# A hybrid attention and MLP layer on one core: tiles at whole kilobytes, longer runs of value products, joined head pairs, relu and square left in PSUM

## The chip, the cores and the metric

The kernel runs on one core of one Trainium2 chip. The metric is device time in microseconds, from the start to the end of one execution; lower is better. Engines are called as in the profile: PE is TensorE's matmul, PEld its weight load, DVE VectorE, ACT ScalarE, POOL GpSimd, SP the engine that issues all DMAs here.

## The reference

One layer of a decoder over 2048 tokens of width 1024, in float32. Cut to what matters:

```python
h = rmsnorm(x, norm_attn)
proj = h @ w_in                       # 2700 columns, for four head groups
# A: stick-breaking attention, 4 heads of 64, strictly causal
# B: sparse attention, 4 heads, one K/V: compressed, selected and window (512) branches,
#    each a softmax with an ALiBi slope, added with sigmoid gates
# C: differential attention, 4 heads: softmax(map 0) - lam * softmax(map 1)
# D: sliding window (128) with sinks, 4 query heads on 2 K/V heads
mix = concat(rmsnorm(A), rmsnorm(B), headnorm(C), rmsnorm(D))
x = x + (mix * g_mix) @ w_out
h = rmsnorm(x, norm_mlp)
x = x + relu(h @ w_up) ** 2 @ w_down  # 4096 wide
return rmsnorm(x, norm_final)
```

## The kernel before

**Dense work.** Each dense product is made of three matmuls on operands split in two: the rounded value (hi) and the rest (lo), as hi*hi, hi*lo and lo*hi. Weights are loaded by SP into one of two `raw` tiles (128 x 1024) and split by ScalarE and by VectorE or GpSimd into `w_hi` and `w_lo` (three of each). Activations stand transposed in `T_hi` and `T_lo`, 128 x 8 x 512, for 512 tokens at a time. Four stages P0 to P3 (`proj`) make the projections; four stages M0 to M3 (`mlp`) make the output projection and the MLP. In M, 32 up projections (`up`) each stream the eight 512-column slices of T against 128-column blocks of w (24 matmuls), and `up_end` makes relu, square, and the split into `u_hi` and `u_lo`: relu out of PSUM into the tile `r`, square in `r`, copy to `u_hi`, all on ScalarE, then the subtraction `u_lo = r - u_hi` on VectorE. Two ups later, down groups of six matmuls stream `w` (512 columns) against 128-column blocks of u, and VectorE adds each group into `acc`. The order is: up, eight down groups, up, and so on. At the end of each M, rows are normed, multiplied with `last_gain` (loaded once, in M0) and stored. These groups share three PSUM banks (`pd`, `PD` = 3); in M3, once all attention is over, the banks of `z` and `t` join them.

**Attention.** For each 128 queries, scores `z` (two matmuls of up to 512 columns) are evicted with slope and mask into `row` tiles, the exponentials are taken there, and an item with the attention's blocks is put in a queue (`item`). The stream `values` takes items in order: four 128 x 128 blocks at a time are transposed into a PSUM tile `t`, which ScalarE evicts into one of `PB` = 3 tiles `PT`. `products` then emits the matmuls of up to `RUN` = 2 such tiles in one go, the last tile first: per block one matmul with 64 columns of V as the stationary operand, which is two instructions in the profile, the two heads of a pair into the two halves of bank `o`'s partitions. A run ends where its item ends, so no run spans two items. In the compressed branch of B and in D each 128 queries have two items, one for each head pair, and `keep_o` evicts 128 columns of `o` for each.

**Order.** One thread of Python generators, called streams, emits all instructions; a planner with a cost of its own for each operation says when a stream's next matmul could start, attention streams go ahead of dense ones, and dense work takes what is left. Each engine then runs its instructions in the order emitted. The planner counts how long a PSUM slot is held.

**Placing in SBUF.** Pools lie one behind the other, tiles rounded up to 32 bytes. The constants begin at byte 16512 of a partition. Over a multiple of 1024 bytes, `T_hi` and `T_lo` begin at 160, `acc` and `nx` at 160, `raw`, `w_hi`, `w_lo`, `u_hi` and `u_lo` at 384, `row`, `qst` (queries), `kst` (keys), `v` and `PT` at 704; slices of T and w begin at multiples of 512 or more from there.

In the profile all matmuls have line 291 (`mm`) or 295 (`tr`), all operations of ScalarE, VectorE and GpSimd line 117, DMAs line 247; tiles are told apart by name. The letter behind `z`, `t` and `o` is the head group, that behind `pd` the stage (P or M). In a matmul's name the moving operand stands ahead of the stationary one.

Of the kernel before, what the change touches and what calls it, by code (L numbers as in the profile page):

```python
# [19 lines left out]
D = 1024  # L20
# [11 lines left out]
QB, RB, PB, WB = 4, 7, 3, 3  # L32
PD, ZB, TB = 3, 2, 2
RUN = 2
# [163 lines left out]
class Trunk:  # L198
# [4 lines left out]
    def __init__(self, ctx, tc, args):  # L203
# [11 lines left out]
        self.dn = ctx.enter_context(tc.tile_pool(name="dn", bufs=1))  # L215
        self.T = (self.dn.tile([128, KD, 512], F32R, name="T_hi", bufs=1),
# [41 lines left out]
    def gains_of(self, name):  # L258

        if name not in self.gain:  # L260
            self.gain[name] = self.const.tile([128, KD], F32, name="gain_" + name)
            self.ld(self.gain[name], dap(getattr(self, name), 0, [[1, 128], [128, KD]]))
        return self.gain[name]
# [37 lines left out]
    def constants(self):  # L301
        V, G, const = self.V, self.G, self.const
        self.ident = const.tile([128, 128], F32, name="ident")
        G.memset(self.ident, 1.0)
        G.affine_select(self.ident, self.ident, [[-1, 128]], OP.is_equal, 0.0, base=0, channel_multiplier=1)
        self.mhalf = const.tile([128, 1], F32, name="mhalf")
        G.memset(self.mhalf, -0.5)
        self.qsc = const.tile([128, 6], F32, name="qsc")
# [17 lines left out]
    def weight_specs(self):  # L326
# [16 lines left out]
        for kind, c in self.phases:  # L343
# [8 lines left out]
            else:  # L352
# [6 lines left out]
                for fc in range(FF // 128 // FC):  # L359
# [4 lines left out]
                    if FC * fc + 3 < FF // 128:  # L364
                        yield kind, c, up(FC * fc + 3)

# [203 lines left out]
    def mlp(self, c):  # L570
# [42 lines left out]
        def up_end(ft, ps):  # L613
# [24 lines left out]
        for fc in range(FF // 128 // FC):  # L638
# [4 lines left out]
            for i in range(4):  # L643
                ts = slice(i * 128, i * 128 + 128)
                ss = self.tile(dn, [128, 2], F32, "nt_ss", 3) if last else None
                for d in range(2):
# [8 lines left out]
                    if last:  # L655
                        r = self.tile(dn, [128, 512], F32, "r", 1)
                        A.activation(r, acc[i][:, ds_], AF.Square, accum_out=ss[:, d:d + 1])
                if last:
                    V.tensor_tensor(ss[:, 0:1], ss[:, 0:1], ss[:, 1:2], OP.add)
                    r = self.rstd(dn, ss[:, 0:1], D, "nt")  # L660
                    for d in range(2):
                        o = acc[i][:, d * 512:d * 512 + 512]
                        V.scalar_tensor_tensor(o, o, r[:, 0:1], self.last_gain[:, d * 512:d * 512 + 512], op0=OP.mult,
                                               op1=OP.mult)
# [11 lines left out]
    def attention_constants(self):  # L676
# [4 lines left out]
        def table(name, w, step, off, window):  # L681
            t = const.tile([128, w], F32, name=name)
# [18 lines left out]
        self.identr = const.tile([128, 128], F32R, name="identr")  # L701
        V.tensor_copy(self.identr, self.ident)

        self.neglam = const.tile([128, 1], F32, name="neglam")
        dl = []
        for a_, b_, nm in ((self.diff_lq1, self.diff_lk1, "l1"), (self.diff_lq2, self.diff_lk2, "l2")):
# [3 lines left out]
            s_ = const.tile([128, 1], F32, name="lams_" + nm)  # L710
            V.tensor_tensor_reduce(u[:, 0, :], u[:, 0, :], u[:, 1, :], 1.0, 0.0, OP.mult, OP.add, s_)
            A.activation(s_, s_, AF.Exp)
            dl.append(s_)
# [3 lines left out]
        self.snk = const.tile([128, 4], F32, name="snk")  # L717
        self.ld(self.snk, dap(self.sinks, 0, [[0, 128], [1, 4]]))
        self.nsnk = const.tile([128, 4], F32, name="nsnk")
# [17 lines left out]
        self.rowok = const.tile([128, 1], F32, name="rowok")  # L737
# [141 lines left out]
    def values(self):  # L879
# [3 lines left out]
        while True:  # L883
# [20 lines left out]
            for g in range(0, nb, 2):  # L904
# [4 lines left out]
                yield self.when([p for P, _ in bl for p in P], "t", TB)  # L909
# [4 lines left out]
                for a, (P, _) in enumerate(bl):  # L914
# [8 lines left out]
                for a, (P, v) in enumerate(bl):  # L923
                    for j in range(len(P)):
                        ops.append((j, v[j], pt[:, 2 * a + j, :], first and g + a == 0, last and g + a == end[j]))
# [650 lines left out]
```

## Time and profile before

| | us |
|---|---|
| median of three timed runs | 3186.9 (3185.98 to 3189.75) |
| the profiled execution, its own time | 3182.32 |
| its span, first to last instruction | 3180.6 |
| PE busy | 3074.8 |
| VectorE busy | 2068.3 |
| ScalarE busy | 1772.9 |
| GpSimd busy | 710.3 |

Busy times are read as shares of the span. A matmul's duration runs from the start of its reading to the end of its result; the next starts long before that, so durations of neighbours overlap, and the distance from one start to the next tells what a matmul costs. In the timeline a row "xN" merges N neighbours of one kind. An attention stage shows as letters A, C, D, B in turn for each 512 queries.

### The profile page before, as it was taken

To read this page: it belongs to the slowest core of one execution; us is meant where nothing else is said; L and a number is where in the kernel's file an instruction comes from. 1 tells how busy PE (TensorE), PEld (TensorE's weight loads), DVE (VectorE), ACT (ScalarE), POOL (GpSimd) and SP (SyncE) were. 2 spreads that over 40 slices of the span, in tenths; PEclk is the share of its full clock that TensorE was granted. 3 is DMA by queue.
4 is the path that set the end of the run, shared out by engine and by line. 5 is a ranking of instruction groups with operands and counts; after the bars stand their busy time and mean duration, and the time that the engine had idled before them with its cause. 6 is when DMAs were issued, how large, how long until landed. Compare 5 with 4: busy or idle time off the path is not lost.

```text
span 3180.6 us, 51156 instructions
## 1 busy us (share of the span) xinstructions
PE 3074.8 (97%) x19152; PEld 2515.3 (79%) x19152; DVE 2068.3 (65%) x4278; ACT 1772.9 (56%) x3459; POOL 710.3 (22%) x479
## 2 busy tenths in 40 slices
PE   8999999999999999989999998999999999999998
PEld 6878887888877777878877776778777778888886
DVE  4774667655758887776566878687665554545545
ACT  4654667554657765656556776566554554333333
POOL 3042313222311222233121112233221112210000
PEclk9999999999999999999999999999999999999999
DMA  7778564765232344364223323452532222423332
GB/s 219 191 196 208 163 164 139 200 179 139 77 94 77 89 112 123 104 175 112 69 75 95 94 75 94 119 168 76 129 110 69 69 69 63 145 86 96 90 100 86
DMA packets 456649, 376.53 MB, mean 118 GB/s; under 512 B 127056, under 2 KB 405712, under 8 KB 454736
## 3 DMA queue, kind: packets, MB, share of 16 engines
q1 hardware_dynamic: 456400, 373.26, 42.6%
q8 instruction: 151, 2.47, 0.3%
q14 instruction: 98, 0.80, 0.1%
HBM read 319.59 MB, written 53.58 MB: 117 GB/s over the span
## 4 chain that ended last, share of the span: by engine, by line
PE 75%; DVE 12%; ACT 6%; DMA 3%; issue 2%; POOL 1%; SPq 1%; DVEq 0%; POOLq 0%; ACTq 0%
PE pdM L291 40%; PE pdP L291 13%; DVE row L117 8%; PE zB L291 4%; PE tB L295 4%; PE oB L291 4%; ACT row L117 4%; PE zC L291 2%; PE oC L291 2%; PE tC L295 2%; DVE acc L117 1%; ACT w_hi L117 1%; DMA raw<-in_w_in_dram 1%; PE tA L295 1%; DMA raw<-in_w_out_dram 1%
## 5 line engine op out<-in xcount | busy, mean ns | idle before, releaser
L117 POOL TENSOR_TENSOR w_lo<-raw,w_hi 128x1024 fp32r<-128x1024 f32 (+1 forms) x188 | 468.6, 2496 | 1363.1 <-ACT w_hi L117 1248.3
L117 ACT ACTIVATE w_hi<-raw 128x1024 fp32r<-128x1024 f32 (+2 forms) x376 | 388.7, 1047 | 462.5 <-PE pdM L291 269.7
L117 DVE TENSOR_TENSOR acc<-acc,pdM 128x512 f32<-128x512 f32 (+1 forms) x576 | 367.8, 652 | 172.3 <-PE pdM L291 162.7
L291 PE MATMUL pdM<-T_lo,w_hi 128*128 128x512 f32 (+1 forms) x1088 | 419.7, 386 | 4.4 <-POOL T_lo L117 4.4
L291 PE MATMUL pdM<-T_hi,w_hi 128*128 128x512 f32 (+1 forms) x1088 | 419.9, 386 | 2.1 <-ACT T_hi L117 1.5
L291 PE MATMUL pdM<-T_hi,w_lo 128*128 128x512 f32 (+1 forms) x1088 | 419.6, 386 | 0.0
L291 PE MATMUL pdM<-w_hi,u_hi 128*128 128x512 f32 x1024 | 405.2, 403 | 8.5 <-DVE acc L117 3.4
L291 PE MATMUL pdM<-w_hi,u_lo 128*128 128x512 f32 x1024 | 405.5, 396 | 3.0 <-DVE u_lo L117 3.0
L291 PE MATMUL pdM<-w_lo,u_hi 128*128 128x512 f32 x1024 | 404.7, 396 | 0.0
L117 DVE TENSOR_TENSOR w_lo<-raw,w_hi 128x1024 fp32r<-128x1024 f32 (+1 forms) x188 | 249.3, 1333 | 220.3 <-ACT w_hi L117 211.9
L117 ACT ACTIVATE row<-row 128x1024 f32<-128x1024 f32 (+7 forms) x292 | 228.6, 803 | 116.3 <-DVE row L117 113.7
L291 PEld LDWEIGHTS pdM<-T_lo,w_hi 128*128 128x128 f32 x1088 | 205.5, 189 | 45.9 <-POOL T_lo L117 5.2
L291 PEld LDWEIGHTS pdM<-T_hi,w_hi 128*128 128x128 f32 x1088 | 205.3, 189 | 42.5 <-ACT T_hi L117 1.8
L291 PEld LDWEIGHTS pdM<-T_hi,w_lo 128*128 128x128 f32 x1088 | 205.6, 189 | 40.3 <-issue 0.5
L291 PEld LDWEIGHTS pdM<-w_hi,u_hi 128*128 128x128 f32 x1024 | 193.1, 189 | 54.1 <-DVE acc L117 8.2
L117 ACT ACTIVATE PT<-tB 128x512 f32<-128x512 f32 (+1 forms) x260 | 134.4, 530 | 168.8 <-PE tB L295 167.2
L291 PEld LDWEIGHTS pdM<-w_hi,u_lo 128*128 128x128 f32 x1024 | 194.1, 190 | 43.2 <-DVE u_lo L117 5.1
L291 PEld LDWEIGHTS pdM<-w_lo,u_hi 128*128 128x128 f32 x1024 | 193.8, 189 | 41.6 <-issue 0.5
L117 ACT ACTIVATE row<-row,c_mn 128x1024 f32<-128x1024 f32 (+4 forms) x192 | 171.6, 896 | 93.3 <-DVE c_mn L117 90.4
L291 PE MATMUL pdP<-T_lo,w_hi 128*128 128x512 f32 x480 | 192.0, 400 | 0.0
L291 PE MATMUL pdP<-T_hi,w_hi 128*128 128x512 f32 x480 | 191.4, 399 | 0.1
L291 PE MATMUL pdP<-T_hi,w_lo 128*128 128x512 f32 x480 | 191.0, 398 | 0.0
(211 smaller groups left out, 6554.4 us busy)
## 6 DMA issues: line engine op xcount, KB each, us to landing
raw<-in_w_up_dram SPq DMA_DIRECT2D x128, 512.0 KB, 4.1
raw<-in_w_down_dram SPq DMA_DIRECT2D x128, 512.0 KB, 3.6
raw<-in_w_in_dram SPq DMA_DIRECT2D x72, 512.0 KB, 5.1
acc<-in_x_dram SPq DMA_DIRECT2D x32, 512.0 KB, 4.8
raw<-in_w_out_dram SPq DMA_DIRECT2D x32, 512.0 KB, 4.5
qst<-qk_qA SPq DMA_DIRECT2D x64, 128.0 KB, 3.4
qst<-qk_qC SPq DMA_DIRECT2D x128, 64.0 KB, 3.4
qst<-qk_qD SPq DMA_DIRECT2D x64, 128.0 KB, 3.2
```

The source lines that it names most:

```text
L117: return f(*a, **k)
L291: self.nc.tensor.matmul(out, a, b, start=start, stop=stop, **k)
L295: self.nc.tensor.transpose(out, a, self.ident[:a.shape[0], :a.shape[0]])
```

## The change

Constants: `PB` from 3 to 6, `RUN` from 2 to 4.

Placing: a tile of the pools `at` and `dn` whose row isn't a multiple of 256 elements goes to a new pool `sm` behind them, as do `gain_*`, `qsc`, `t_cmp` and `rowok`; `ident` and `identr` become one tile, the lambda sums one, `snk` and `nsnk` one, and `last_gain` leaves the constants. The constants are then 12160 bytes, and 16512 + 12160 = 28672 is 28 KB, so that all large tiles (T, w, u, raw, acc, nx, row, qst, kst, v, PT) begin at a multiple of 1 KB.

Items: a block gets a third part `m`, the column block of `o` into which its products go. The compressed branch and D make one item for both head pairs; `keep_o` gets the pair of bounds and evicts 256 columns at once.

MLP: relu and square stay in the PSUM tile `ps`, and `u_hi` and `u_lo` are made from it; the tile `r` is gone, and the squares for the last norm are written to `ps` too. `norm_final` is loaded at the end of every M stage through a `raw` tile, which is given back at the fourth block of rows.

```diff
-QB, RB, PB, WB = 4, 7, 3, 3
+QB, RB, PB, WB = 4, 7, 6, 3
-RUN = 2
+RUN = 4
...
     def tile(self, pool, shape, dt, name, bufs, tag=None):
+
+        if pool in (self.at, self.dn) and math.prod(shape[1:]) % 256:
+            pool = self.sm
...
-        self.ident = const.tile([128, 128], F32, name="ident")
-        G.memset(self.ident, 1.0)
-        G.affine_select(self.ident, self.ident, [[-1, 128]], OP.is_equal, 0.0, base=0, channel_multiplier=1)
+        one = self.row_tile()[:, :128]
+        G.memset(one, 1.0)
+        G.affine_select(one, one, [[-1, 128]], OP.is_equal, 0.0, base=0, channel_multiplier=1)
+        self.identr = const.tile([128, 128], F32R, name="identr")
+        V.tensor_copy(self.identr, one)
+        self.ident = self.identr.bitcast(F32)
...
+                yield "G", c, [(lambda t: t, dap(self.norm_final, 0, [[0, 128], [1, D]]))]
...
+            if self.rawq[0][0] == "G":
+                self.wq.append(self.rawq.pop(0)[2])
+                continue
             yield from self.res["w"].take()
...
-        if c == 0:
-            self.last_gain = self.const.tile([128, D], F32, name="last_gain")
-            self.ld(self.last_gain, dap(self.norm_final, 0, [[0, 128], [1, D]]))
...
-            r = self.tile(dn, [128, 512], F32, "r", 1)
-            A.activation(r, ps, AF.Relu)
-            A.activation(r, r, AF.Square)
-            A.activation(uh, r, AF.Copy)
-            V.tensor_tensor(ul, r, uh.bitcast(F32), OP.subtract)
+            A.activation(ps, ps, AF.Relu)
+            A.activation(ps, ps, AF.Square)
+            A.activation(uh, ps, AF.Copy)
+            V.tensor_tensor(ul, ps, uh.bitcast(F32), OP.subtract)
...
-                        r = self.tile(dn, [128, 512], F32, "r", 1)
-                        A.activation(r, acc[i][:, ds_], AF.Square, accum_out=ss[:, d:d + 1])
+                        A.activation(ps, acc[i][:, ds_], AF.Square, accum_out=ss[:, d:d + 1])
...
+                    if i == 0:
+                        gain, = yield from self.weights()
...
                     self.res["acc"].give()
+                    if i == 3:
+                        self.res["raw"].give()
...
-        for n, (j, v, p, _, _) in enumerate(ops):
-            self.mm(o[64 * j:64 * j + 64, 0:128], v, p, n == starts[j], n == stops[j], share=2)
+        for n, (j, m, v, p, _, _) in enumerate(ops):
+            self.mm(o[64 * j:64 * j + 64, 128 * m:128 * m + 128], v, p, n == starts[j], n == stops[j], share=2,
+                    skip_group_check=True)
...
-                self.item(blocks, [self.vcn], [], self.keep_o(box, "c", pr),
-                          rel=(lambda: self.res["pc"].give()) if pr else None)
+
+            def blocks(vc, pc=pc):
+                return [((pc[:, 2 * m, 0:128], pc[:, 2 * m + 1, 0:128]), (vc, vc), m) for m in range(2)]
+
+            self.item(blocks, [self.vcn], [], self.keep_o(box, "c", (0, 2)), rel=lambda: self.res["pc"].give())
...
-            self.evac(box[nm][:, 128 * pr:128 * pr + 128], o[:, :128])
-            if pr and then:
+            self.evac(box[nm][:, 128 * p0:128 * p1], o[:, :128 * (p1 - p0)])
+            if p1 == 2 and then:
                 self.final(then())
...
-                self.item(blocks, [("vD", c, g)], [], self.keep_o(box, "d", g, f),
-                          rel=(lambda: self.give_rows(1)) if g else None)
+            self.item(blocks, [("vD", c, g) for g in range(2)], [], self.keep_o(box, "d", (0, 2), f),
+                      rel=lambda: self.give_rows(1))
```

## Rows read from the trace of the kernel before

**Rows 1.** The page: the span, its first part (busy time, share and instructions of each engine), and the first line of its fourth part, the chain that ended last, by engine.

```profile
span 3180.6 us, 51156 instructions
...
PE 3074.8 (97%) x19152; PEld 2515.3 (79%) x19152; DVE 2068.3 (65%) x4278; ACT 1772.9 (56%) x3459; POOL 710.3 (22%) x479
...
PE 75%; DVE 12%; ACT 6%; DMA 3%; issue 2%; POOL 1%; SPq 1%; DVEq 0%; POOLq 0%; ACTq 0%
```

**Rows 2.** The view of waits, PE alone: who waited for whom, us in total, times, and the longest.

```profile
PE zC L291 <- DVE c_mn L117: 12.6, 13, 3.1
...
PE zA L291 <- ACT row L117: 6.3, 8, 2.1
...
PE pdM L291 <- DVE acc L117: 4.0, 8, 1.1
...
PE pdM L291 <- ACT u_hi L117: 3.4, 2, 2.3
...
PE pdM L291 <- DVE u_lo L117: 3.0, 4, 1.1
```

**Rows 3.** The timeline of PE in three short stretches, each with a run of products between dense or score matmuls: start, duration, what, and how many.

```profile
2354.25 0.39 PE L291 MATMUL pdM<-w_hi,u_lo 128*128 128x512 f32 x1
2354.57 0.44 PE L291 MATMUL oB<-PT,vcn 128*64 128x128 f32 x4
2354.94 0.50 PE L291 MATMUL pdM<-w_lo,u_hi 128*128 128x512 f32 x1
2355.27 0.40 PE L291 MATMUL pdM<-w_hi,u_hi 128*128 128x512 f32 x1
...
1063.37 0.39 PE L291 MATMUL pdM<-w_lo,u_hi 128*128 128x512 f32 x1
1063.69 1.09 PE L291 MATMUL oA<-PT,v 128*64 128x128 f32 x16
1064.71 0.73 PE L291 MATMUL zA<-kst,qst 128*128 128x512 f32 x2
...
2395.46 0.40 PE L291 MATMUL pdM<-T_lo,w_hi 128*128 128x512 f32 x1
2395.79 1.31 PE L291 MATMUL oB<-PT,v 128*64 128x128 f32 x20
2397.03 0.73 PE L291 MATMUL zB<-kst,qst 128*128 128x512 f32 x2
```

**Rows 4.** The timeline of PE in M3: the first and the last of 15 up matmuls in a row (14 distances), and the first and the last of 38 down matmuls in a row (37 distances).

```profile
2851.20 0.40 PE L291 MATMUL pdM<-T_hi,w_hi 128*128 128x512 f32 x1
...
2854.47 0.40 PE L291 MATMUL pdM<-T_hi,w_lo 128*128 128x512 f32 x1
...
2856.55 0.39 PE L291 MATMUL pdM<-w_lo,u_hi 128*128 128x512 f32 x1
...
2864.94 0.39 PE L291 MATMUL pdM<-w_lo,u_hi 128*128 128x512 f32 x1
```

**Rows 5.** The groups of PE's instructions by shape: one of the three groups of each dense kind with 512 columns (the other two have the same counts); count, busy time, mean of one, idle time before them.

```profile
L291 PE MATMUL pdM<-w_hi,u_hi 128*128 128x512 f32 x1024 | 405.2, 403 | 8.5 <-DVE acc L117 3.4 <-ACT u_hi L117 3.4 <-ACT r L117 1.1
...
L291 PE MATMUL pdM<-T_hi,w_hi 128*128 128x512 f32 x960 | 382.8, 399 | 0.6 <-DVE acc L117 0.6
...
L291 PE MATMUL pdP<-T_lo,w_hi 128*128 128x512 f32 x480 | 192.0, 400 | 0.0
```

**Rows 6.** The groups by shape, of ScalarE and of VectorE: the four steps behind an up projection in M, and the like two on a projection in P, which read PSUM.

```profile
L117 ACT ACTIVATE u_hi<-r 128x512 fp32r<-128x512 f32 x128 | 81.0, 632 | 2.5
L117 ACT ACTIVATE r<-r 128x512 f32<-128x512 f32 x128 | 80.9, 632 | 2.4
...
L117 ACT ACTIVATE r<-pdM 128x512 f32<-128x512 f32 x128 | 74.7, 584 | 8.9 <-PE pdM L291 4.5 <-DVE u_lo L117 4.4
...
L117 ACT ACTIVATE u_hi<-pdP 128x512 fp32r<-128x512 f32 x32 | 18.7, 583 | 4.2 <-PE pdP L291 4.2
...
L117 DVE TENSOR_TENSOR u_lo<-r,u_hi 128x512 fp32r<-128x512 f32 x128 | 97.5, 762 | 76.5 <-ACT u_hi L117 76.5
...
L117 DVE SCALAR_TENSOR_TENSOR u_lo<-pdP,u_hi 128x512 fp32r<-128x512 f32 x32 | 21.9, 685 | 10.3 <-ACT u_hi L117 10.3
```

**Rows 7.** The timelines of PE, ScalarE and VectorE around one up projection in M1: its last matmul, the relu, the copy to u_hi, and the subtraction.

```profile
1605.91 0.40 PE L291 MATMUL pdM<-T_hi,w_lo 128*128 128x512 f32 x1
...
1607.74 0.57 ACT L117 ACTIVATE r<-pdM 128x512 f32<-128x512 f32 x1
...
1609.54 0.63 ACT L117 ACTIVATE u_hi<-r 128x512 fp32r<-128x512 f32 x1
...
1610.98 0.69 DVE L117 TENSOR_TENSOR u_lo<-r,u_hi 128x512 fp32r<-128x512 f32 x1
```

**Rows 8.** The page's sixth part (DMA issues: count, size, median us from issue to landing), and the view by tile: duration shortest, median and longest, first and last start. The transposes of group B's outputs, the last of attention, over the whole span; the matmuls on w_out in a stretch about the start of M3.

```profile
raw<-in_w_out_dram SPq DMA_DIRECT2D x32, 512.0 KB, 4.5
...
L295 PE MATMUL tB<-ident,oS x96: 270/273/332, 336.1 to 2693.4; 128*128 128x128 f32 x96
...
L291 PE MATMUL pdM<-w_hi,T_hi x128: 277/280/285, 2753.3 to 2803.9; 128*128 128x256 f32 x128
```

More of the change, by code (lines that the diff above doesn't have):

```diff
@@ L260, in gains_of @@
         if name not in self.gain:
-            self.gain[name] = self.const.tile([128, KD], F32, name="gain_" + name)
+            self.gain[name] = self.sm.tile([128, KD], F32, name="gain_" + name)
             self.ld(self.gain[name], dap(getattr(self, name), 0, [[1, 128], [128, KD]]))
@@ L681, in table @@
         def table(name, w, step, off, window):
-            t = const.tile([128, w], F32, name=name)
+            t = (self.sm if name == "t_cmp" else const).tile([128, w], F32, name=name)
             for o, n in self.pieces(0, w, 512):
@@ L908, in values @@
                 yield from self.res["PT"].take()
-                yield self.when([p for P, _ in bl for p in P], "t", TB)
+                yield self.when([p for P, _, _ in bl for p in P], "t", TB)
                 self.pa = pa
@@ L913, in values @@
                 n = 0
-                for a, (P, _) in enumerate(bl):
+                for a, (P, _, _) in enumerate(bl):
                     for j in range(len(P)):
@@ L922, in values @@
                 ops = []
-                for a, (P, v) in enumerate(bl):
+                for a, (P, v, m) in enumerate(bl):
                     for j in range(len(P)):
-                        ops.append((j, v[j], pt[:, 2 * a + j, :], first and g + a == 0, last and g + a == end[j]))
+                        ops.append((j, m, v[j], pt[:, 2 * a + j, :], first and g + a == 0, last and g + a == end[j]))
                 if run and (len(run) == RUN or run[-1][-2]):
@@ L932, in products @@
         pa, obox, _, _, first, _, _ = run[0]
-        yield self.when([x for r in run for x in [r[2]] + [v for _, v, _, _, _ in r[3]]], "o" if first else None, 1)
+        yield self.when([x for r in run for x in [r[2]] + [v for _, _, v, _, _, _ in r[3]]], "o" if first else None, 1)
         self.pa = pa
@@ L1125, in blocks @@
                     return [((blk(b),) + ((blk(b + 1),) if b < i else ()),
-                             (v[:, b, :],) + ((v[:, b + 1, :],) if b < i else ())) for b in range(0, i + 1, 2)]
+                             (v[:, b, :],) + ((v[:, b + 1, :],) if b < i else ()), 0) for b in range(0, i + 1, 2)]
                 def fin(o, i=i, h=h, rc=rc, t=t):
@@ L1339, in blocks @@
                     return [((P[0][:, b * 128:b * 128 + 128], P[1][:, b * 128:b * 128 + 128]),
-                             (v[:, b0 + b, :], v[:, b0 + b, :])) for b in range(nb)]
-                self.item(blocks, [("vw", c)], [], self.keep_o(box, "w", pr), rel=lambda: self.give_rows(2))
+                             (v[:, b0 + b, :], v[:, b0 + b, :]), 0) for b in range(nb)]
+                self.item(blocks, [("vw", c)], [], self.keep_o(box, "w", (pr, pr + 1)), rel=lambda: self.give_rows(2))
             segs = self.pieces(0, n, 1024)
@@ L1483, in sinks_window, with blocks, f @@
-                self.item(blocks, [("vD", c, g)], [], self.keep_o(box, "d", g, f),
-                          rel=(lambda: self.give_rows(1)) if g else None)
+            def blocks(*v, rw=rw, b0=b0, nb=w // 128):
+                return [((rw[:, 2 * g, b * 128:b * 128 + 128], rw[:, 2 * g + 1, b * 128:b * 128 + 128]),
+                         (v[g][:, b0 + b, :], v[g][:, b0 + b, :]), g) for g in range(2) for b in range(nb)]
+            def f(box=box, mn=mn, sm=sm, t=t, i=i):
+                if t == 3:
+                    self.res["v"].give(2)
+                es = self.small(4, "d_es")
+                V.tensor_tensor(es, self.snk, mn, OP.add)
+                A.activation(es, es, AF.Exp)
+                V.tensor_tensor(sm, sm, es, OP.add)
+                V.reciprocal(es, sm)
+                s_ = box["d"]
+                yield self.when([s_], "t", TB)
+                self.pa = pa
+                ps = self.tt()
+                for r in range(2):
+                    self.tr(ps[:, r, :], s_[:, r * 128:r * 128 + 128])
+                self.res["oS"].give()
+                on = self.on_tile()
+                V.tensor_tensor(on.rearrange("p (h d) -> p h d", d=64),
+                                ps[:, 0:2, :].rearrange("p r (j d) -> p (r j) d", d=64),
+                                es[:, :, None].to_broadcast([128, 4, 64]), OP.mult)
+                self.group_norm_store(on, i, 3)
```

65 lines of the change are left out of this document (17 added, 48 removed).

## The prediction

> **What bounds the kernel now.** I read the page first: of a span of 3180.6 us TensorE (PE) is busy for 3074.8, VectorE for 65% and ScalarE for 56%, and 75% of the chain that ended last lies on PE [rows 1]. A busy PE need not be a PE at its peak, so I read next what PE waited for: the largest entries shown are 12.6 us for scores on VectorE's minima and 6.3 for scores on rows, and the waits of the MLP on its own evictions are 4.0, 3.4 and 3.0 us [rows 2]. So PE has nearly always something to issue, attention or dense work, and time is won where PE's own work shrinks. That can happen in two ways: fewer or cheaper switches between kinds of matmul, and shorter distances between matmuls of one kind. For both I read PE's timeline and take distances from start to start, since durations overlap.
>
> The profiled execution took 3182.3 us (span 3180.6); the median of the three timed runs is 3186.9, 4.6 above it. I make the sum on the profiled one and add the 4.6 at the end.
>
> **Value runs of up to four banks.** Each product is two instructions, four for a block of two heads. The timeline has product runs of 4, 16 and 20 instructions between matmuls of 512 columns [rows 3]. From start to next start: run of 4, 0.37 us (2354.57 to 2354.94); 16, 1.02 (1063.69 to 1064.71); 20, 1.24 (2395.79 to 2397.03). The slopes are 0.65/12 = 0.054 and 0.22/4 = 0.055 us, so four instructions are 0.218 of the 0.37, and 0.152 is fixed. The run's start also comes 0.32 us after the dense matmul ahead of it, where 0.227 is usual (0.093 more), and the first matmul behind the run of 4 takes 0.33 (0.103 more). Together a run costs 0.348 us of PE whatever its length.
>
> How many runs go, I count from the code. A run never spans two items, so an item of b banks has ceil(b/2) runs before and ceil(b/4) after. Stick-breaking: 40 to 24 for each of 2 head pairs. Differential: 24 to 16 for each of 4 heads. Selected branch: 40 to 24 for each of 2 pairs; window branch: 28 to 16 for each of 2. Compressed branch, two items of one block made one: 32 to 16. Sinks: 32 to 16. The sum is 376 to 224, 152 less. Some runs stand back to back today already and cost nothing extra, as the 20 do, which is a run of 16 and one of 4 [rows 3]; I take off a tenth, an estimate. 152 x 0.9 x 0.348 = **48 us less**. All of it is PE time, and nothing hides it. The bounds: 30 us if a third already stands back to back, 53 if none does.
>
> Behind a longer run waits what PE does next, at most 32 instructions instead of 16, another 0.9 us; PE itself loses nothing by that, but VectorE and ScalarE get a score later. The value stream's last bank is still being evicted when a run is emitted, as now; the planner lets other work go first. Six PT buffers leave two beyond a run of four, so no transpose waits for a product. One eviction for two heads' pairs in place of two saves ScalarE time, which bounds nothing here.
>
> **SBUF at multiples of 1 KB.** An up projection streams T (it begins 160 bytes over a multiple of 1 KB) against blocks of w; a down projection streams w (384 bytes over) against blocks of u. Both are 128 x 512 in the same type. In the last stage the up matmuls start every (2854.47 - 2851.20)/14 = 0.2336 us and the down ones every (2864.94 - 2856.55)/37 = 0.2268 [rows 4]. The difference of 6.8 ns holds over long stretches where nothing is waited for. After the change T, w, u, kst and qst all begin at whole kilobytes, so T lies at least as evenly as w does now, and T and w stand to each other as w and u do now. Either way of seeing it gives T the spacing of w. There are 3 x 960 such matmuls in M and 3 x 480 in P [rows 5]: 4320 x 6.8 ns = **29 us less**. That the address makes the difference is my inference; the trace of before has no T at another address. Bounds: nothing, if something else sets the two apart; 50 us more, if going from multiples of 128 bytes to 1 KB is worth another such step for all 4320 + 3072 matmuls of 512 columns. I take the 29 because the row of w is the nearest.
>
> A rule speaks against this term. In the Trainium skill, SBUF — State Buffer, section "SBUF: two separate sides", TensorE has read ports of its own and never waits on another reader. By it the tile's place could buy nothing and the sum would lack this term; it leaves unexplained why the two spacings differ in rows 4.
>
> **Relu and square in PSUM.** Before, an up's bank is free when the relu has been read out of it; after, when VectorE has made u_lo. ScalarE gets faster: an activation out of PSUM takes 584 ns, one from SBUF 632, so the square falls by about 48 and the copy to 583, as u_hi from pdP has it; the subtraction goes from 762 to about 685, as the like one from pdP [rows 6]. That is 0.17 us off a chain that PE hardly waits for: nothing on the end. The price is the bank. In one up of M1 the last matmul starts at 1605.91 and ends about 1606.30; the relu is over at 1608.31, u_lo at 1611.67 [rows 7]. The bank is held 5.4 us instead of 2.0. There are three such banks, and the down groups that follow (six matmuls of 0.227, 1.36 us) then rotate over two. The planner knows the hold and issues attention meanwhile, and in M3, once attention is done, the z and t banks join: 32 of the 128 ups cost nothing. For the other 96 I let today's waits on acc, u_hi and u_lo, 10.4 us [rows 2], nearly double: **8 us more**. Bounds: 0 (cover holds), and 3.4 us x 96 = 326 if nothing covers.
>
> **The gain vector through the raw buffers.** It is loaded once per M stage instead of once, and holds one of two raw buffers until the fourth block of the last group. The next stage's w_out tiles, queued behind it on SP, come in through one buffer. A load lands in 4.5 us [rows 8]. At two of the three borders attention runs and covers; at the last, M2 to M3, nothing does (the last attention transpose is at 2693.4, the first matmul on w_out at 2753.3 [rows 8]). **4 us more**, between 0 and three landings, 14.
>
> **The rest.** Identity from one tile, merged small constants, and u, r and gains in other pools change no instruction of weight. The one added hop at the start (identity cast on VectorE) lies beside the first loads. With 77 us less PE work, VectorE's and ScalarE's chains have less time: their shares rise by a fortieth, and PE will wait a bit oftener. I give back a tenth, **7 us**. More is not likely: attention ends 60 us before M3 begins to use it, so its pace may lag by most of the gain before the end moves.
>
> **Sum.** -48 - 29 + 8 + 4 + 7 = -58; 3182.3 - 58 = 3124, and with the 4.6 **3129 us**. With its own uncertainties 3112 to 3150.
>
> **Rivals.**
> First, the spacing of T has another cause than the address. Then 29 us stay away: 3158. For it: no row shows one tile at two addresses. Against: same shape, type and count, and a steady difference.
>
> Second, whole kilobytes are worth more than w's place now: another 6.8 ns on 7392 matmuls, 50 us, gives 3079. For it: w's 0.2268 us need not be the floor. Against: no row has a 512-column stream that runs steadily faster.
>
> Third, slower than before: the pd bank becomes the bound. Each of 96 ups holds its bank 3.4 us longer; if PE idles one of them, 96 us come in place of the 8, and 3129 - 8 + 96 = 3217. It decides from 0.7 us per up, where 66 us and the 8 eat the gain. For it: three banks, a VectorE queue with instructions of over a microsecond ahead of u_lo. Against: today's waits on these evictions are 4.0 us in all [rows 2], and attention stands ready in these stages. The Trainium skill bears on it: ScalarE: Activation LUTs, "Step-by-step: what each stage is for", calls PSUM the quicker place for ScalarE but useful only where TensorE doesn't need most of PSUM. [...]
>
> Fourth, the change does not make longer runs, because the value stream flushes when its queue is empty. It flushes between items only, and the count above takes that in; I give it no chance of its own.
>
> **How the numbers follow.** Forecast 0.56, first rival 0.22, second 0.13, third 0.09. The likeliest gives 3129. The range reaches down past the second rival with less costs, 3070, and up to the first with its costs doubled, 3158 + 19, say 3180; the third, and what lies below, is left out. A measurement of this kernel tells about 0.2% (6.4 us) from no change: slower than 3193 is most of the third rival, 0.08; within 3180.5 to 3193 fall its mild form and the first rival's worst, 0.05; faster 0.87.
>
> **What would show it.** Runs right: product runs of up to 32 instructions between dense matmuls, 0.35 us fixed each. Alignment right: up matmuls start every 0.227 us, not 0.234; lower still for both kinds would be the second rival. Banks wrong: PE's waits on VectorE's u_lo and acc in the hundreds. Gain vector: a wait on raw from w_out near the start of M3. The forecast is wrong if T still starts every 0.234 us, or if PE's waits grow by more than 40 us.

## The result, and the profile after

The changed kernel takes 3163.4 us in the median of six runs (3159.16 to 3167.26), against 3186.4 of the kernel before: a ratio of 0.9925, 95% interval 0.9912 to 0.9939. That is 23 us less, where 58 were forecast. The direction is right, the size less than half. The profiled execution took 3159.2 us.

The page of the changed kernel, its span and first part, which answer to [rows 1]:

```profile
span 3157.4 us, 50995 instructions
...
PE 3027.8 (96%) x19152; PEld 2533.0 (80%) x19152; DVE 2072.5 (66%) x4278; ACT 1760.3 (56%) x3410; POOL 714.3 (23%) x479
```

The view of cores of the same kernel, span and mean granted clock:

```profile
core 0: 3157.4 us, clock 0.989
```

PE's busy time fell by 47.0 us (3074.8 to 3027.8); its idle time, span less busy, rose from 105.8 to 129.6, by 23.8. Their sum is the 23 us. The forecast had 77 us less work and 19 us of costs. The clock record of the traces divides the busy time further. PE was busy for 47.3 us in stretches of half clock (1.2 of 2.4 GHz) before, and for 56.4 after. Counted at full rate, that is with half of these stretches taken off, PE's work fell from 3051.2 to 2999.6 us, by 51.6, and half clock cost 4.6 more than before.

PE's waits in the changed kernel (us in total, times, longest), which answer to [rows 2]:

```profile
PE pdM L296 <- DVE acc L117: 14.9, 13, 3.1
...
PE pdM L300 <- DVE nx L117: 10.6, 3, 7.0
PE zC L296 <- DVE c_mn L117: 10.2, 12, 3.0
PE zA L296 <- ACT row L117: 8.9, 12, 1.5
PE pdM L296 <- ACT u_hi L117: 6.3, 4, 3.4
PE pdM L296 <- DVE u_lo L117: 5.6, 7, 1.9
```

The three waits of the MLP on its own evictions (acc, u_hi, u_lo) went from 10.4 to 26.8 us, and one wait of 7.0 us on nx, between M3's output projection and its first up, is new.

PE's timeline in M3: the first and last of 48 up matmuls in a row, then of 38 down matmuls; they answer to [rows 4]:

```profile
2848.71 0.39 PE L296 MATMUL pdM<-T_hi,w_hi 128*128 128x512 f32 x1
...
2859.36 0.39 PE L296 MATMUL pdM<-T_hi,w_lo 128*128 128x512 f32 x1
```

```profile
2840.10 0.39 PE L296 MATMUL pdM<-w_lo,u_hi 128*128 128x512 f32 x1
...
2848.48 0.39 PE L296 MATMUL pdM<-w_lo,u_hi 128*128 128x512 f32 x1
```

Ups now start every 10.65/47 = 0.2266 us, downs every 8.38/37 = 0.2265: T has the spacing of w, and neither went lower.

A long run of products in M1, and four transposes without a run ahead of them, which answer to [rows 3]:

```profile
1062.33 0.39 PE L296 MATMUL pdM<-T_lo,w_hi 128*128 128x512 f32 x1
1062.65 1.97 PE L296 MATMUL oA<-PT,v 128*64 128x128 f32 x32
1064.55 0.66 PE L300 MATMUL tA<-identr,row 128*128 128x128 f32 x4
1064.96 0.71 PE L296 MATMUL zA<-kst,qst 128*128 128x512 f32 x2
```

```profile
964.01 0.60 PE L300 MATMUL tB<-identr,row 128*128 128x128 f32 x4
964.36 0.42 PE L296 MATMUL zA<-kst,qst 128*128 128x128 f32 x2
```

From the dense matmul to the transposes are 2.22 us. Less 0.227 for the dense matmul and 32 x 0.0545 for the products, 0.25 are left; the four transposes behind the run take 0.41 instead of 0.35. A run ahead of transposes thus costs 0.31 us, not the 0.348 read between dense matmuls. Counted over PE's whole timeline, neighbouring product rows taken together, there were 398 runs before and are 264 now. Of the 134 that went, 104 had a transpose behind them (235 before, 131 after).

The MLP's evictions in the changed kernel, grouped by shape (ScalarE's relu and square together, its copy, VectorE's subtraction), which answer to [rows 6]:

```profile
L117 ACT ACTIVATE pdM<-pdM 128x512 f32<-128x512 f32 x256 | 149.2, 583 | 12.6 <-PE pdM L296 10.1
L117 DVE TENSOR_TENSOR u_lo<-pdM,u_hi 128x512 fp32r<-128x512 f32 x128 | 87.7, 686 | 64.5 <-ACT u_hi L117 64.2
L117 ACT ACTIVATE u_hi<-pdM 128x512 fp32r<-128x512 f32 x128 | 76.3, 597 | 2.6
```

583, 597 and 686 ns, where some 584, 583 and 685 were forecast. One side in PSUM is enough for ScalarE: before, relu took 584 from PSUM into SBUF, and the last norm's square, whose source `acc` lies in SBUF, went from 631 into SBUF to 591 into PSUM. One up in M1, its last matmul, relu, square, copy and subtraction, which answer to [rows 7]:

```profile
1605.78 0.39 PE L296 MATMUL pdM<-T_hi,w_lo 128*128 128x512 f32 x1
...
1606.99 0.58 ACT L117 ACTIVATE pdM<-pdM 128x512 f32<-128x512 f32 x1
1607.78 0.59 ACT L117 ACTIVATE pdM<-pdM 128x512 f32<-128x512 f32 x1
1608.40 0.60 ACT L117 ACTIVATE u_hi<-pdM 128x512 fp32r<-128x512 f32 x1
...
1611.16 0.68 DVE L117 TENSOR_TENSOR u_lo<-pdM,u_hi 128x512 fp32r<-128x512 f32 x1
```

The bank is held from 1606.17 to 1611.84, 5.7 us, where 5.4 were forecast.

SP's issues about the border from M2 to M3 in the changed kernel, and the view of windows there (us, busy time of PE, PEld, DVE, ACT and POOL with their instructions, granted clock, DMA share, GB/s), which answer to [rows 8]:

```profile
2713.94 0.33 SPq L252 DMA_DIRECT2D raw<-in_norm_final_dram  x1
2716.20 0.38 SPq L252 DMA_DIRECT2D raw<-in_w_out_dram  x1
...
2723.03 0.38 SPq L252 DMA_DIRECT2D raw<-in_w_out_dram  x1
...
2744.22 0.43 SPq L252 DMA_DIRECT2D raw<-in_w_out_dram  x1
```

```profile
2710.00:2735.00 25.00, 20.93 (x99) 17.08 (x98) 12.93 (x20) 12.22 (x23) 13.48 (x10) 0.93 0.38 126
2735.00:2760.00 25.00, 21.98 (x160) 21.29 (x159) 13.46 (x23) 6.71 (x12) 2.52 (x4) 0.93 0.73 232
2760.00:2785.00 25.00, 25.00 (x210) 25.00 (x210) 10.34 (x19) 6.54 (x8) 1.10 (x2) 1.00 0.37 107
2785.00:2810.00 25.00, 18.01 (x142) 17.77 (x141) 10.32 (x16) 10.02 (x15) 12.39 (x10) 0.86 0.13 43
```

The same issues in the kernel before:

```profile
2734.31 6.28 SPq L247 DMA_DIRECT2D raw<-in_w_out_dram  x3
...
2763.30 1.53 SPq L247 DMA_DIRECT2D raw<-in_w_out_dram  x2
```

The gain vector does take a raw buffer: behind it only two w_out tiles are issued ahead of a pause of 21 us. But the pause is not the gain's: before, three tiles were issued and then came one of 23 us. And idle time is paid twice: where PE waits (busy for 18.01 of 25 us), the granted clock falls as well (a mean of 0.86; 1.00 where PE is busy throughout). There the clock is at half from 2792.0 to 2798.8, and the wait on nx ends at 2795.97.

### The profile page after: what moved, and what is told of

Same layout as the page of the kernel before. It is cut to its first block, busy times and chain, and to the rows that moved or that the text cites. A ratio compares the mean times of both kernels' runs of the same rounds, so it can differ in the third digit from the quotient of the medians.

```text
span 3157.4 us, 50995 instructions
## 1 busy us (share of the span) xinstructions
PE 3027.8 (96%) x19152; PEld 2533.0 (80%) x19152; DVE 2072.5 (66%) x4278; ACT 1760.3 (56%) x3410; POOL 714.3 (23%) x479
## 4 chain that ended last, share of the span: by engine, by line
PE 49%; DVE 10%; ACT 5%; DMA 2%; issue 2%; POOL 0%; SPq 0%; DVEq 0%; ACTq 0%; POOLq 0%
PE pdM L296 36%; DVE row L117 7%; ACT row L117 3%; PE zB L296 2%; PE tB L300 2%; PE oB L296 2%; PE zC L296 1%; DVE acc L117 1%; PE tC L300 1%; PE oC L296 1%; ACT w_hi L117 1%; PE oA L296 1%; DMA raw<-in_w_out_dram 0%; PE pdM L300 0%; DVE w_lo L117 0%
```

## The experiments

Each was timed beside the kernel before, whose median was 3185.2 to 3186.5 us in these comparisons. The planner writes a new order for nearly every edit. The three kernels with another placing alone, and the one with five PT buffers, keep PE's order of their base but for 0 to 36 of its 19152 instructions; the others differ from theirs in some 1,900 to 5,500.

The theory going in (theory 1) was that the bank's hold by relu and square costs much more than the 8 us forecast. Its rivals: the gain vector's load (theory 2), and long runs that give their gain back in waits (theory 3).

### The placing

The kernel before with its tiles at multiples of 1 KB:

```diff
+        self.sm = ctx.enter_context(tc.tile_pool(name="sm", bufs=1))
+        pad = self.const.tile([128, 80], F32, name="pad")
...
+        if pool in (self.at, self.dn) and math.prod(shape[1:]) % 256:
+            pool = self.sm
```

> The kernel before with nothing but the placing changed: a pad of 320 bytes behind the constants and the small tiles in a pool of their own, so that T, w, u, raw, acc, nx, row, qst, kst, v and PT begin at multiples of 1 KB; instructions in the same order up to a few dozen. If the tile's place sets the spacing of T and PE is the bound: up matmuls every 0.227 us instead of 0.2336 and 25 to 29 us less than before, 3158 to 3162. If PE's freed time is lost to waits: 10 to 15 us less. If the place does nothing: no change.

3167.7 us (0.9944, 0.9931 to 0.9956): 18 less, between the first two expectations. PE busy 3058.3, idle 106.4, so hardly any of the freed time went to waits. The first and last of 26 ups in M3 are 5.67/25 = 0.2268 us apart:

```profile
2854.45 0.39 PE L296 MATMUL pdM<-T_hi,w_hi 128*128 128x512 f32 x1
...
2860.12 0.39 PE L296 MATMUL pdM<-T_lo,w_hi 128*128 128x512 f32 x1
```

With one order the two traces can be laid beside each other, matmul by matmul. 3856 of the 4320 ups are followed, at full clock and without a wait, by another up. Their distances sum to 911.4 us before and 893.3 here: 18.1 less, 4.7 ns each. The downs gain 3.1 us. The 256-column matmuls lose 4.0: the median of their distances goes from 0.117 to 0.120 us.

Then the changed kernel with T at a multiple of 1 KB, and everything behind it 32 bytes on (384 in the second, with 96 columns for the 8):

```diff
+        pad = self.dn.tile([128, 8], F32, name="pad", bufs=1)
```

> The changed kernel (3163) with one tile of 32 bytes put behind T: T stays at a multiple of 1 KB, and acc, nx, raw, w and u lie 32 bytes over one. The order of PE's instructions stays. Theory A, a moving operand's own address decides, and 32 bytes over a multiple of 64 is what is slow: up matmuls (T moving) stay at 0.227 us, down matmuls (w moving) go from 0.227 to about 0.233; 3072 of them at 5.4 to 6.8 ns are 17 to 21 us, so 3180 to 3184. Theory B, the place of T against w decides, as both explain the kernel before: ups go back to 0.233, downs stay at 0.227, and what the alignment gave is lost, 18 us: 3181. The total does not tell A from B, the two spacings do. Theory C, neither matters: 3163 and no spacing moves.

> As the kernel with w 32 bytes on, but with 384 bytes behind T: acc, nx, raw, w and u lie 384 bytes over a multiple of 1 KB, as raw, w and u did in the kernel before; T stays at 0. Theory A, a multiple of 64 is all that counts: ups and downs both at 0.227, 3163. Theory B, the place of T against w decides: ups at 0.233, 3181. Theory D, whole kilobytes slow the matmuls of 256 columns, which start every 0.1195 us in the changed kernel and every 0.117 in the one before: they go back to 0.117, and 2688 of them at 2.5 ns give 6.7 us, 3156.

3181.0 us (0.9987, 0.9978 to 0.9997) and 3180.3 (0.9980, 0.9969 to 0.9991). M3 with 32 bytes, 48 ups and then 44 downs:

```profile
2861.95 0.40 PE L298 MATMUL pdM<-T_hi,w_hi 128*128 128x512 f32 x1
...
2872.92 0.40 PE L298 MATMUL pdM<-T_hi,w_lo 128*128 128x512 f32 x1
```

```profile
2829.89 0.39 PE L298 MATMUL pdM<-w_hi,u_lo 128*128 128x512 f32 x1
...
2839.63 0.39 PE L298 MATMUL pdM<-w_lo,u_hi 128*128 128x512 f32 x1
```

and with 384 bytes, 48 ups:

```profile
2861.65 0.40 PE L298 MATMUL pdM<-T_hi,w_hi 128*128 128x512 f32 x1
...
2872.61 0.39 PE L298 MATMUL pdM<-T_hi,w_lo 128*128 128x512 f32 x1
```

Ups are back at 10.97/47 = 0.2334 and 10.96/47 = 0.2332 us, though T has not moved; downs, whose w and u both moved, stay at 9.74/43 = 0.2265. Theory B holds: what counts is where T stands against w, the moving operand against the stationary one, and 17 to 18 us hang on it. Theory D falls: with 384 bytes the 256-column matmuls don't go back to 0.117 us but to 0.119. With 32 bytes they do go back, though, so their pace too hangs on the places, and not in the way of the ups. These three comparisons are firm, since the order is the same.

### Relu and square: PSUM or SBUF

The tile r back, paid for with one PT buffer; and the changed kernel with five PT buffers alone:

```diff
-QB, RB, PB, WB = 4, 7, 6, 3
+QB, RB, PB, WB = 4, 7, 5, 3
...
-            A.activation(ps, ps, AF.Relu)
-            A.activation(ps, ps, AF.Square)
-            A.activation(uh, ps, AF.Copy)
-            V.tensor_tensor(ul, ps, uh.bitcast(F32), OP.subtract)
+            r = self.tile(dn, [128, 512], F32, "r", 1)
+            A.activation(r, ps, AF.Relu)
+            A.activation(r, r, AF.Square)
+            A.activation(uh, r, AF.Copy)
+            V.tensor_tensor(ul, r, uh.bitcast(F32), OP.subtract)
```

> The changed kernel with relu and square taken back into the SBUF tile r (one buffer); PB is 5 to make room. The dense matmuls of M wait 28 us longer in the changed kernel than before, and the planner, which counts the hold of a PSUM bank, places dense work elsewhere. Theory 1 (the pd bank held through relu, square, copy and subtraction ate the gain): 15 to 25 us less than the changed kernel (3163), some 3140, and PE's waits on acc and u_hi fall from 21 us back to about 8. Theory 2 (the gain vector in the raw buffer) or theory 3 (long runs delay attention): within 5 us of the changed kernel.

> The changed kernel (3163) with five PT buffers in place of six; relu and square stay in PSUM. The kernel with the tile r in SBUF has five too, for want of room, so its 18 us may belong to the buffers. Theory 1, the PSUM bank's hold: 3163 to 3166, the fifth buffer alone changes little. Rival, a sixth buffer lets transposes run ahead and take PE from other work at a bad time: 3145 to 3150, and the hold costs nothing.

3145.3 us (0.9873, 0.9859 to 0.9887) and 3165.0 (0.9931, 0.9915 to 0.9946). So the bank seemed to cost 18 to 20 us; the fifth buffer changes nothing, not even PE's order. But the waits did not fall as expected: acc and u_hi together went from 21.2 to 11.5 us, not to 8, and all three from 26.8 to 19.7. The same edit the other way in the kernel before, and in that one aligned:

> The kernel before (3186) with one edit: relu and square of an up projection stay in PSUM, and the tile r goes. Theory 1, the bank that is held until u_lo is made costs PE what it cost in the changed kernel, 18 us: 3204, with waits of dense matmuls on VectorE's acc grown from 4 us to 10 or more. The forecast's term: 8 us, 3194. Theory 3, the hold costs only where runs are long, since they keep ScalarE and VectorE busier: 3186 to 3190.

> The kernel before with its tiles at multiples of 1 KB (3168) and relu and square in PSUM. At the old placing this edit cost some 5 us, in the changed kernel some 18. Theory 1a, it is the faster PE that bares the hold, since down groups come sooner to a bank: 3168 + 15, some 3183. Theory 1b, it is the joined items and the rest of the change that bare it: 3168 + 5, some 3173.

3191.1 us (1.0017, 1.0007 to 1.0026) and 3174.1 (0.9959, 0.9944 to 0.9974): 5 and 6 more than their bases, though the waits on acc grew as the theory has it (4.0 to 14.6 us, 3.6 to 15.9). No theory so far gave both 18 and 5.

### Runs and items

Runs of two (`RUN = 2`) in the changed kernel, and with r in SBUF:

> The changed kernel with RUN = 2 (PB stays 6, joined items stay). By the fixed 0.348 us per run, some 120 runs come back: 42 us more than the changed kernel, 3205, if the long runs earn what was forecast. Theory 3 (long runs keep the chain of scores waiting and give the gain back): only 10 to 20 us more, 3175 to 3183, and PE's waits on scores and rows fall.

> The kernel with relu and square in the SBUF tile r and five PT buffers (3145), and runs of at most two PT tiles in place of four. It is the long runs' worth where no PSUM bank is held by the MLP's squares. Theory 1, runs are worth what PE's busy time fell by (31 us from runs of two to four in the changed kernel) and half of it was lost there to waits on held banks: 3145 + 27 to 31, 3172 to 3176. Theory 2, longer runs give only some 16 us wherever they stand, since they cost waits of their own: 3145 + 16 = 3161. The forecast's price, 0.348 us for each run, would give 3145 + 40 = 3185.

3179.9 us (0.9982, 0.9970 to 0.9993) and 3159.3 (0.9922, 0.9908 to 0.9935): with runs of four the time is 16 and 14 lower, each time between two orders. PE's busy time falls by 31.4 (3059.2 to 3027.8, 115 runs fewer) and 31.1 (3053.4 to 3022.3, 98 fewer), 0.27 and 0.32 us a run; at full rate its work falls by 29.9 and 23.7, 0.26 and 0.24 a run. Idle time grows by 14 in both, and the waits on scores, which theory 3 had fall with short runs, are about the same (22.3 us with runs of two, 23.8 with four). Runs of three with r in SBUF:

> The kernel with r in SBUF and runs of up to three PT tiles; with two it takes 3159, with four 3145. Theory 1, PE's own saving and its longer waits both grow with the runs' length: between the two, 3150 to 3154. Theory 2, the waits come from runs of four alone, with one spare buffer of five: 3140 to 3144. Theory 3, the waits come already with three and the fewer runs don't: 3159 or more.

3157.3 us (0.9908, 0.9890 to 0.9925); PE busy 3031.9, idle 119.1 against 103.4 with runs of two and 117.5 with four. The work falls with each step, the idle time jumps at the first. Then the two branches with an item for each head pair again, with r in SBUF and with PSUM:

```diff
-                return [((pc[:, 2 * m, 0:128], pc[:, 2 * m + 1, 0:128]), (vc, vc), m) for m in range(2)]
-            self.item(blocks, [self.vcn], [], self.keep_o(box, "c", (0, 2)), rel=lambda: self.res["pc"].give())
+            for m in range(2):
+                def blocks(vc, pc=pc, m=m):
+                    return [((pc[:, 2 * m, 0:128], pc[:, 2 * m + 1, 0:128]), (vc, vc), 0)]
+                self.item(blocks, [self.vcn], [], self.keep_o(box, "c", (m, m + 1)),
+                          rel=(lambda: self.res["pc"].give()) if m else None)
```

(and the same for D).

> The kernel with r in SBUF (3145), and the compressed branch and the sinks with an item for each head pair again, as in the kernel before; runs of up to four. Theory 1, joined items earn 0.35 us for each of the 32 runs that they save, on the path in full: 3145 + 11 = 3156, which is also what is left between the aligned kernel before and the one with runs of two when alignment and the gain vector are taken off. Rival, they earn nothing that shows (the branches are small and their runs stand back to back with others): 3145 to 3148, and the 11 us belong to something else.

> The kernel with r in SBUF and an item for each head pair (3161), with relu and square in PSUM. The hold of the bank cost 5 to 6 us in the two kernels with the old items, whose gain vector is loaded once, and 18 to 20 in those with joined items and a gain load in each stage. If joined items bare it: 3161 + 5, some 3166. If the gain load, or the rest of the new kernel, does: 3161 + 18, some 3179.

3160.7 us (0.9922, 0.9907 to 0.9937) and 3171.8 (0.9948, 0.9936 to 0.9961). With joined items the time is 15 us lower with r in SBUF and 7 in PSUM (3171.8 to 3165.0); PSUM is 11 slower here, between both expectations. These are differences of two orders too, so what joined items earn in time is not shown; PE's work at full rate falls by 10.2 and 16.0.

### The gain vector

No load of the gain; the last multiplication reads a table that is there anyway, so the output lacks the final norm's gain:

```diff
-                yield "G", c, [(lambda t: t, dap(self.norm_final, 0, [[0, 128], [1, D]]))]
...
-                        V.scalar_tensor_tensor(o, o, r[:, 0:1], gain[:, d * 512:d * 512 + 512], op0=OP.mult,
+                        V.scalar_tensor_tensor(o, o, r[:, 0:1], self.t_causal[:, d * 512:d * 512 + 512], op0=OP.mult,
```

> The changed kernel without the loads of norm_final: the last product takes a slice of a constant table of the same shape instead, so the output lacks the final gain; no raw buffer is held at the end of an M stage. Theory 2 (the held raw buffer starves the next stage's w_out): 10 to 15 us less than the changed kernel, most of it between 2700 and 2800 us, where PE waits 3.0 us on w_hi and 7.0 on nx. Theories 1 and 3: 0 to 5 us less.

3160.8 us (0.9921, 0.9907 to 0.9936), 2.6 below the changed kernel, where theory 2 had 10 to 15. The order differs as well, so the time alone decides little. Between 2690 and 2830 us PE's waits are 14.0 us in the changed kernel and 9.3 without the load; the 3.0 on w_hi are gone, the 7.0 on nx stay. But they are 10.0 with r in SBUF, where the gain is loaded too. Theory 2 falls as the large cost; whether the load costs anything is not shown.

### The order

Does the added idle time come from a plan that is too tight? A margin of 0.5 us with runs of four and of two, and a hop of 0.35 in the third:

```diff
-    HOP, MARGIN = 0.15, 0.1
+    HOP, MARGIN = 0.15, 0.5
```

> The kernel with r in SBUF, runs of four (3145, PE idle 117 us of its span), and the planner's margin from 0.1 to 0.5 us: an attention matmul is taken only when its operands have been ready for that long by the plan, and dense work goes first. The plan counts nothing for the start of a run, so each run that goes takes 0.35 us of unplanned time from ScalarE and VectorE. Theory W, the waits that long runs add come from an order planned too tight: PE's idle time falls by 8 to 14 and the time to 3131 to 3138. Rival, VectorE and ScalarE lack the capacity in these stages: the waits only move, 3143 to 3150.

> The kernel with r in SBUF and runs of two (3159, PE idle 103 us of its span), with the same margin of 0.5 us. Theory W: here the unplanned 0.35 us of many runs already give the slack, so the margin brings little, 3155 to 3160, and runs of four beat runs of two by some 25 us once both have it. Rival: the margin helps both alike, or neither, and the difference stays at 14.

> The kernel with r in SBUF, runs of four (3145), and the time that the planner counts from one engine's result to another's start from 0.15 to 0.35 us, for dense work and for the chains of ScalarE and VectorE too. Theory W: a plan that is less tight everywhere takes away waits on acc and u_lo as well; 3130 to 3140. Rival, no capacity: 3143 to 3150.

3143.0 us (0.9858, 0.9843 to 0.9873), 3183.5 (0.9990, 0.9981 to 0.9999) and 3162.1 (0.9917, 0.9903 to 0.9931). PE's idle time is 120.2, 122.5 and 132.7 us: more slack in the plan gave more idle time, not less. Theory W falls. A loss of 24 us from a margin, with runs of two (3159.3 to 3183.5), fits no theory, so the last question was what an order alone is worth. Margin 0.12 in place of 0.10, with r in SBUF and in the changed kernel:

> The kernel with r in SBUF (3145) with the planner's margin from 0.10 to 0.12 us, a change too small to mean anything but another order of instructions. It measures how far an order alone moves the time. If the order is a small matter: 3142 to 3148. If it is not, this kernel lies 5 us or more from 3145.

> The changed kernel (3163) with the planner's margin from 0.10 to 0.12 us, beside the same edit of the kernel with r in SBUF. If the hold of the PSUM bank costs 18 us whatever the order, this one lies 15 to 20 us above that one. If the 18 were in part the luck of two orders, the difference is under 10 or over 25, and the cost of the hold is known only as a mean over pairs: 18, 20 and 11 so far in the new kernel's pairs.

3157.9 us (0.9918, 0.9904 to 0.9932) and 3146.0 (0.9872, 0.9855 to 0.9890). The one got 13 us slower, the other 17 faster, and their sign is turned round: here PSUM is 12 us faster. The page's first part, with r in SBUF and margin 0.10, and the view of its cores:

```profile
PE 3022.3 (96%) x19152; PEld 2527.3 (80%) x19152; DVE 2059.9 (66%) x4278; ACT 1766.4 (56%) x3410; POOL 714.0 (23%) x479
```

```profile
core 0: 3139.8 us, clock 0.992
```

The same two with margin 0.12:

```profile
PE 3036.7 (96%) x19152; PEld 2539.8 (80%) x19152; DVE 2068.7 (66%) x4278; ACT 1767.0 (56%) x3410; POOL 718.3 (23%) x479
```

```profile
core 0: 3156.1 us, clock 0.986
```

And the page's first part of the changed kernel with margin 0.12, whose span is 3147.1 us at a clock of 0.989:

```profile
PE 3021.7 (96%) x19152; PEld 2529.7 (80%) x19152; DVE 2056.9 (65%) x4278; ACT 1760.6 (56%) x3410; POOL 709.8 (23%) x479
```

Between the first two nearly all of the 16.3 us of span are busy time (14.4), and that is the clock: PE was busy at half clock for 37.4 and 68.8 us, half of the difference is 15.7, and at full rate the work is 3003.6 and 3002.3. But these are single executions. The granted clock changes from one execution of a kernel to the next (0.988 to 0.992 in the four with margin 0.10, 0.986 to 0.990 in the six with 0.12), and at 0.988 and 0.989 the first kernel took 3147.8 and 3146.5, the second 3155.9 and 3158.0. So 8 to 12 of the 13 us are there at one clock as well, and their cause is not shown. The profiled executions of the changed kernel's two orders are 10 us apart, not 17: 6 of them busy time and 4 idle, with one clock. So the theory that the bank's hold costs 18 us falls: that pair compared two orders. What can be said of the hold is a mean over six pairs, PSUM less SBUF: 20 (with five PT buffers in both), 21, 11, -12, 5, 6, on average 8 with an uncertainty of some 5 (their scatter is 12; the last two pairs have nearly the same orders and count for little more than one). That alone doesn't tell 8 from nothing. PE's idle time is steadier: 14, 13, -1, 6, 4, 6 more in PSUM, on average 7 with an uncertainty of some 2.

## Why the prediction was right in direction and wrong in size

**Alignment, 29 forecast, 18 measured: the mechanism right, the term mis-sized.** The spacing did go from 0.2336 [rows 4] to 0.2266 us in M3, as forecast, and the first rival falls; that the time lies near its 3158 is chance. The step that failed is the price: 6.8 ns were read in a steady stretch of M3 and taken for all 4320 matmuls. In the kernel with another placing alone the mean distance of neighbouring ups (those less than 0.26 us apart, at full clock) falls from 0.2331 to 0.2267 us behind 2800 us, where no attention is left, but only from 0.2330 to 0.2287 ahead of it. Over the 3856 neighbours it is 4.7 ns, 18.1 us. The other ups have a transpose, a score, a run or a wait behind them and gain little more than 1 us together: ahead of a transpose the median is 0.231 before and 0.232 after. The sum also left out the 256-column matmuls, which lost 4.0 us; the downs gained 3.1. PE's work at full rate fell by 16.7. Why the gain is smaller beside attention is open. "T and w stand to each other as w and u do now" was the right one of the two reasons given. What the Trainium skill says in SBUF — State Buffer, "SBUF: two separate sides", of other readers on which TensorE never waits, no run here shows; where TensorE's own two operands stand to each other was worth 4 to 7 ns a matmul, and of that the section says nothing.

The second rival (whole kilobytes worth more) falls with 0.2265 us as the lowest steady spacing seen, and with the 256-column matmuls, which got slower.

**Runs and items, 48 forecast, 35 measured.** The difference was counted right, 134 runs fewer for 137, but partly by luck: there were 398 and 264 runs, where the code gave 376 and 224. The step that failed is the price again. It was read from one run of four between dense matmuls, and three quarters of the runs that went stood ahead of transposes, where 0.31 is read. The whole trace gives less than either: from the aligned kernel to the changed one PE's work at full rate fell from 3034.5 to 2999.6, by 34.9 us, 0.26 for each run. For runs of two to four, in pairs, it fell by 29.9, 23.7 and 38.4 us (0.26, 0.24 and 0.34 a run), the time by 16, 14 and 41 (the third pair with margin 0.5). This measure hardly depends on the order: it moved by 1.2 and 3.1 us between two orders of one kernel. The forecast's lower bound, a third back to back, is 152 x 2/3 x 0.348 = 35, not 30.

**Costs, 19 forecast (8, 4 and 7), 28 measured in this order.** 23.8 are idle time; 4.6 are half clock, which the forecast left out. Relu and square in PSUM agree with the forecast's 8 on average, in time (8, uncertain by 5) and in PE's idle time (7, uncertain by 2), and in no order they cost what the third rival gave. That rival's "4.0 us in all" is the wait on acc alone; the three waits are 10.4, as the term itself had it. The gain vector, 4, can't be told from nothing. The tenth given back to waits, 7, is the weakest term: with longer runs PE's idle time grew by 14 in two pairs and shrank by 2 in a third.

**The sum.** Of the 35 us between the forecast's 58 and the measured 23, 12 are the alignment term (29 less 16.7), 13 the runs and items (48 less 34.9), 5 the idle time and 5 half clock.

**The order, not forecast at all.** Any edit here makes the planner write another order, and two orders of one kernel differ by 13 and 17 us. The changed kernel is one draw; with the margin at 0.12 the same kernel takes 3146, 39 less than before instead of 23.

What stays open: why longer runs raise PE's idle time in some orders (neither more margin nor one more PT buffer took it away), what the two orders of one kernel differ by at one clock, and whether the kernel before is a lucky or an unlucky draw; no other order of it alone was timed.

## What to carry to other kernels

Read a spacing in every stage where its matmuls stand before you take it as a price for all of them, not in the steadiest stretch alone, and count the other shapes that a new placing touches; and read the price of a switch ahead of the operation that follows it most often, not in the tidiest example. In a program that a planner orders, time the same kernel under a second order before giving any difference under some 20 us a cause: a comparison of times is firm only if the order stays. Where it can't stay, divide the time into PE's work at full rate, half clock and idle time, and compare each. Give the two operands of a 512-column matmul the same place over a multiple of 1 KB, and look at both together, not at each alone; the 256-column matmuls here lost by it, so count both kinds.

## What the runs showed of the hardware that was not expected

TensorE's pace in fp32r depends on where its two SBUF operands stand to each other: in steady stretches 0.2266 us for 512 columns when both are 0 (or both 32 or 384) bytes over 1 KB, 0.2332 to 0.2336 with 0 against 32, 0 against 384, or 160 against 384. For 256 columns it is another way round: a median of 0.120 us with both at 0, 0.119 with 0 against 384, 0.117 with 0 against 32 or 160 against 384. In the stretches read, a run of column-tiled products costs 0.25 us to enter and leave; the transposes behind it take another 0.06, dense matmuls another 0.10. Over whole executions each run less saved 0.24 to 0.34. And PE's waits cost more than their length: before and after the change every stretch of half clock but the one at the very end begins during a wait of PE or within 2 us of its end. PE was busy at half clock for 31.9 to 68.8 us in the profiled executions, and half of that is lost.
